# A decoder layer whose down projection is reordered feature by feature, with earlier weight fetches

## The chip, the cores and the metric

The kernel runs on one core of one Trainium2 chip. Its time is the device time of one execution in microseconds (us). Five engines work beside each other, each on its own queue of instructions in a fixed order: TensorE (PE in the profile; PEld is its weight load), VectorE (DVE), ScalarE (ACT), GpSimd (POOL) and SyncE (SP), which here only issues transfers (DMAs). GpSimd issues transfers too, those that add what they bring to what is there.

## The reference

The layer takes x (512 tokens of 1024 features, float32) and computes three sub-layers, each between two RMS norms: a SwiGLU feed-forward part, a token mixing part, and a second feed-forward part. The change touches the two feed-forward parts alone; cut to them the reference is:

```python
def swiglu(x, w_gu, w_down):                 # w_gu: 1024 x 5632, w_down: 2816 x 1024
    g, u = jnp.split(x @ w_gu, 2, axis=-1)
    return (jax.nn.silu(g) * u) @ w_down

h = h + 0.5 * rmsnorm(swiglu(rmsnorm(h, ffn1_pre_w), ffn1_w_gu, ffn1_w_down), ffn1_post_w)
u = rmsnorm(h, mix_pre_w)
h = h + rmsnorm(token_mixing(u, mem, ...), mix_post_w)       # untouched by the change
h = h + 0.5 * rmsnorm(swiglu(rmsnorm(h, ffn2_pre_w), ffn2_w_gu, ffn2_w_down), ffn2_post_w)
```

## The kernel before

**Precision.** TensorE is used with operands rounded to a short float32 form. Each operand is split in two, `hi` (a copy by ScalarE) and `lo` (the remainder, a subtraction by VectorE; `split`, L171 to L173), and each product is three matmuls, hi by hi, hi by lo, lo by hi (`mm3`, L377). So each 128x512 piece of a weight costs one ScalarE and one VectorE instruction before it can be used.

**A feed-forward part** (`ffn`, L713) has 22 groups of 128 hidden features ("features" below). The first two (EARLY) are computed in the plain way at the start ("heads"). The other 20 go in five *wides* of four. In a wide (`wide_pair`, L642) gate and up columns are computed with Strassen's scheme: the 2x2 block product is made of seven products, numbered 1 to 7 and run in the order 1, 6, 2, 5, 7, 4, 3, each of 24 matmuls of 512 columns (`wide_product`, L629). Their left operands are halves of the normalised x and sums of these (`xhi`, `xlo`, t1 to t4). Their right operands are blocks of w_gu or sums of blocks (`wide`, L584): products 1, 2 and 4 use blocks as loaded (tiles `st`, four buffers); products 5 and 7 use sums of two blocks, made by a plain load from SyncE and an accumulating one from GpSimd onto it (tiles `sum`, five buffers, `both`, L593); products 6 and 3 use a block of which VectorE adds one of these in place. Split pieces lie in 18 buffers `w`. The loads of a product are issued from up to four products before it.

**Turning.** The results of a wide have tokens in rows, and the down projection needs features in rows. `turn` (L694) does this for each of the four groups of 128 tokens: VectorE transposes 32x32 blocks (L698), a transfer writes to DRAM (L701), another reads back with rows exchanged (L704), and ScalarE and VectorE split the result (L709, L710). Before the change VectorE reads its input with a step of four elements, the write is one transfer of 128 rows, and the exchange of rows lies in the read.

**Down projection.** The features of one wide are multiplied by their rows of w_down during the next wide, between its products (`downs`, L807). For each half of the 1024 output columns it takes all (two or four) weight pieces of 128x512, each through one of two staging buffers `sh` and split into the common pool of 37 slots (names `s`), and then goes token group by token group: one of three PSUM banks `px`, all features of this group (3 matmuls each), and one addition to the result `y` by VectorE (for the first two features a copy by ScalarE). `DOWNS` (L44) says how many such steps follow each product, one row for common wides, one for the last wide of the second part, one for that of the first. The last features go behind the last wide with weights of their own (four in the second part; six in the first, where two of the wide before are kept back, `tail`), loaded as `st` and split into `w` buffers and into the places of t1 to t4, which are free by then (`spare`). Then the norm and the residual sum follow for each token group.

**What sets the order.** The kernel is a Python program that issues instructions in the order in which it runs; generators let steps of one task stand between those of another. A scheduler then fixes the order on each engine ahead of time: among the instructions that would be ready by its own estimate of durations, the one issued earliest by the program goes first. So an instruction can stand behind another that is late in fact. Loads go through `bring` (L148); right after the start the first nine are held in their order (`ordered`, L577). The beginning of the kernel (`open`, L464) is written out in a fixed order; there the reciprocal root of each norm is a GpSimd instruction (L194).

Of the kernel before, what the change touches and what calls it, by code (L numbers as in the profile page):

```python
# [8 lines left out]
F32 = mybir.dt.float32  # L9
# [34 lines left out]
DOWNS = ((0, 1, 1, 1, 2, 1, 2), (0, 1, 1, 1, 1, 1, 1), (0, 1, 1, 1, 1, 0, 0))  # L44
# [3 lines left out]
EARLY = 2  # L48
# [3 lines left out]
class Layer:  # L52
# [531 lines left out]
    def wide(self, w, c1, c2):  # L584


        k0 = w.rearrange("(k p) c -> p k c", p=P)
        raw, ops = {}, {}

        def quarter(j, h, c):  # L590
            raw[j] = [x[:, i, :] for x in (self.load(w, 4 * h + 2 * n, 2, c, 512) for n in range(2)) for i in range(2)]

        def both(j, h1, d1, h2, d2):  # L593
            raw[j] = []
            for k in range(4):
                u = self.wpool.tile([P, 512], F32, tag="sum", bufs=NSUM, name=f"sum{self.uid()}")
                self.bring(u, k0[:, 4 * h1 + k, d1:d1 + 512])
                self.nc.gpsimd.dma_start(out=u, in_=k0[:, 4 * h2 + k, d2:d2 + 512], accum_op=ALU.add)  # L598
# [95 lines left out]
    def turn(self, g, turned, t):  # L694
# [3 lines left out]
        self.nc.vector.transpose(blocks.rearrange("p (b f i) -> p f b i", b=4, f=4), g.rearrange("p (f j b) -> p f b j", f=4, b=4))  # L698
        n = self.uid()
        d = self.dram.tile([4, 32, 4, P], F32, tag=f"turn{n}", name=f"turn{n}")  # L700
        self.nc.sync.dma_start(out=d.rearrange("a j b x -> (a j) (b x)"), in_=blocks)  # L701
# [11 lines left out]
    def ffn(self, w_gu, w_down, w_post, ready, reload, after, early, last=False):  # L713
# [26 lines left out]
        def down_weights(f, hf):  # L740

            st = self.stage.tile([P, 512], F32, tag="st2", bufs=2, name=f"sh{self.uid()}")
            self.bring(st, w_down[f * P:(f + 1) * P, HALVES[hf]])
            return self.wsplit(st, slot=True)

        def down(t, hf, act, ws, first, bank=self.paux, cs=slice(0, 512)):
            acc = bank((P, cs.stop - cs.start))
            lhs = act(t)
            for k in range(len(ws)):
                self.mm3(acc, lhs[k], (ws[k][0][:, cs], ws[k][1][:, cs]), k == 0, k == len(ws) - 1)  # L750
            if first:
                nc.scalar.copy(y[t][hf], acc)
            else:
                self.tt(y[t][hf][:, cs], y[t][hf][:, cs], acc, ALU.add)

        wides = [self.wide(w_gu, f * P, DFF + f * P) for f in range(early, NF, 4)]
# [57 lines left out]
        tail = 0 if last else 2  # L814
        f0, n, act = 0, early, of_heads
        for s in range(len(wides)):
# [18 lines left out]
        ws, spare = [], list(self.spare())  # L835
        for j in range(n):
            st = self.load(w_down, f0 + j, 1, 0, D)
            ws.append([])
            for hf in range(2):
                i = j - 2 + (n - 2) * hf  # L840
                if j < 2 or i >= len(spare):
                    ws[-1].append(self.wsplit(st[:, 0, HALVES[hf]]))
                else:
                    self.split(*spare[i], st[:, 0, HALVES[hf]])
                    ws[-1].append(spare[i])
# [3 lines left out]
        if last:  # L849
            self.last_tiles(lambda t, hf, cs: down(t, hf, act, [w[hf] for w in ws], False, self.psum, cs), y, gain, h, after)  # L850
            return tasks
        for t in range(NT):
            whole, parts = slice(0, 512), (slice(0, 256), slice(256, 512))
            ss = []
            for hf in range(2):
                for cs in parts if hf == 1 and t == NT - 1 else (whole,):
                    down(t, hf, act, [w[hf] for w in ws], False, self.psum, cs)
# [692 lines left out]
```

## Time and profile before

| what | value |
|---|---|
| three runs | 1370.13, 1376.26, 1377.42 us (median 1376.26) |
| the profiled execution | 1378.38 us, its span 1376.6 us |
| mean granted clock of TensorE | 0.991 of full speed |
| busy: PE, DVE, ACT, POOL | 1324.1, 1053.1, 728.1, 94.8 us |
| matmuls | 7548 |
| bytes moved | 206.01 MB |

The first feed-forward part takes about the first 385 us of the span, the mixing the time up to about 1020 us, the second feed-forward part the rest. In the views a row of a timeline is: start and duration in us, engine, line, operation, written tile and the tiles it reads, shape, count, and in brackets the idle time of the engine before it with what ended that. "SPq" and "POOLq" are the issuing of transfers. Names such as s, w, st, sum, sh, px, ps are those of the tiles above, without their numbers (px and ps are PSUM).

### The profile page before, as it was taken

How to read it: one execution, taken by the hardware profiler on the slowest of the kernel's cores; microseconds unless marked ns; L12 is line 12 of the kernel's file. 1: busy time of each engine (PE TensorE's matmuls, PEld its weight loads, DVE VectorE, ACT ScalarE, POOL GpSimd, SP SyncE). 2: the span in 40 equal slices, each digit the busy share in tenths (PEclk: the TensorE clock that was granted, in tenths of full speed). 3: DMA queues.
4: the chain of work that ended last, by engine and by line, in shares of the span. 5: the costliest groups of instructions: out<-in, count | busy, mean ns of one | idle time of the engine just before them, and what ended most of it. 6: DMA issues, size and time to landing. Idle time of an engine off the chain costs nothing.

```text
span 1376.6 us, 21006 instructions
## 1 busy us (share of the span) xinstructions
PE 1324.1 (96%) x7548; PEld 1146.9 (83%) x7548; DVE 1053.1 (76%) x1911; ACT 728.1 (53%) x1457; POOL 94.8 (7%) x124
## 2 busy tenths in 40 slices
PE   7989899999899999999999999999999999999996
PEld 7867777778679898899889999999788877777785
DVE  5777768687799886599958978897577969586776
ACT  6555354444367765365765655565465644443442
POOL 2012020200010000000000000001001020101000
PEclk9999999999999999999999999999999999999998
DMA  9368384937725344343314333327625694857534
GB/s 269 100 184 227 126 225 128 243 123 192 253 77 142 121 129 145 106 133 110 106 47 123 95 99 93 111 90 184 214 92 133 180 253 121 231 157 194 154 115 161
DMA packets 190055, 206.01 MB, mean 150 GB/s; under 512 B 12761, under 2 KB 120702, under 8 KB 189950
## 3 DMA queue, kind: packets, MB, share of 16 engines
q1 hardware_dynamic: 174006, 180.47, 41.5%
q0 software_dynamic: 11520, 20.98, 9.2%
q10 hardware_dynamic: 4424, 3.22, 0.7%
q8 instruction: 59, 0.97, 0.3%
q14 instruction: 46, 0.38, 0.1%
HBM read 184.67 MB, written 19.96 MB: 149 GB/s over the span
## 4 chain that ended last, share of the span: by engine, by line
PE 58%; DVE 17%; DMA 15%; ACT 4%; issue 3%; POOL 1%; SPq 0%; POOLq 0%; DVEq 0%; ACTq 0%
PE ps L380 14%; PE ps L398 7%; PE ps L399 6%; PE ps L400 6%; PE px L380 6%; DVE s L167 6%; DVE w L167 4%; DMA sh<-in_ffn_w_down_dram 4%; PE ps L638 4%; PE ps L637 4%; PE ps L639 4%; PE px L385 4%; DMA sum<-in_ffn_w_gu_dram 3%; DVE s L698 2%; PE px L389 2%
## 5 line engine op out<-in xcount | busy, mean ns | idle before, releaser
L172 ACT ACTIVATE w<-st 128x512 fp32r<-128x512 f32 x360 | 219.8, 628 | 135.7 <-PE ps L638 52.1
L167 DVE TENSOR_TENSOR w<-st,w 128x512 fp32r<-128x512 f32 x368 | 245.4, 686 | 24.3 <-ACT w L172 21.4
L380 PE MATMUL px<-s,s 128*128 128x512 f32 x816 | 210.2, 397 | 24.0 <-ACT s L172 22.8
L167 DVE TENSOR_TENSOR w<-sum,w 128x512 fp32r<-128x512 f32 x208 | 142.2, 688 | 96.8 <-ACT w L172 93.4
L380 PEld LDWEIGHTS px<-s,s 128*128 128x128 f32 x816 | 152.5, 190 | 69.2 <-ACT s L172 31.4
L172 ACT ACTIVATE w<-sum 128x512 fp32r<-128x512 f32 x208 | 128.6, 631 | 135.3 <-DMA sum<-in_ffn_w_gu_dram 65.9
L167 DVE TENSOR_TENSOR s<-s,s 128x512 f32<-128x512 f32 (+3 forms) x277 | 169.5, 621 | 29.8 <-ACT s L672 17.4
L598 POOL DMA_DIRECT2D sum<-in_ffn_w_gu_dram x80 | 70.4, 949 | 876.8 <-DVE w L167 438.5
L167 DVE TENSOR_TENSOR s<-s,ps 128x256 f32<-128x256 f32 (+1 forms) x155 | 86.9, 560 | 32.4 <-PE ps L380 27.8
L398 PE MATMUL ps<-xhi,w 128*128 128x256 f32 x384 | 108.9, 284 | 0.0
L400 PE MATMUL ps<-xhi,w 128*128 128x256 f32 x384 | 108.7, 283 | 0.0
L399 PE MATMUL ps<-xlo,w 128*128 128x256 f32 x384 | 108.6, 283 | 0.0
L638 PE MATMUL ps<-w,xhi 128*128 128x512 f32 x240 | 93.9, 391 | 0.6 <-DVE w L167 0.6
L637 PE MATMUL ps<-w,xhi 128*128 128x512 f32 x240 | 93.5, 391 | 0.4 <-ACT w L172 0.4
L639 PE MATMUL ps<-w,xlo 128*128 128x512 f32 x240 | 93.5, 390 | 0.0
L380 PE MATMUL ps<-s,w 128*128 128x512 f32 (+1 forms) x384 | 80.2, 364 | 0.0
L380 PE MATMUL ps<-w,xhi 128*128 128x512 f32 x256 | 80.0, 393 | 0.0
L398 PEld LDWEIGHTS ps<-xhi,w 128*128 128x128 f32 x384 | 73.6, 192 | 0.7 <-ACT s L407 0.2
L399 PEld LDWEIGHTS ps<-xlo,w 128*128 128x128 f32 x384 | 73.6, 192 | 0.6
L380 PEld LDWEIGHTS ps<-s,w 128*128 128x128 f32 x384 | 65.0, 189 | 10.7
L400 PEld LDWEIGHTS ps<-xhi,w 128*128 128x128 f32 x384 | 73.6, 192 | 0.0
L172 ACT ACTIVATE s<-sh 128x512 fp32r<-128x512 f32 x68 | 42.8, 632 | 57.5 <-DMA sh<-in_ffn_w_down_dram 57.5
(234 smaller groups left out, 3081.5 us busy)
## 6 DMA issues: line engine op xcount, KB each, us to landing
st<-in_ffn_w_gu_dram SPq DMA_DIRECT2D x68, 512.0 KB, 5.2
st<-in_w_in_dram SPq DMA_DIRECT2D x48, 512.0 KB, 3.7
sum<-in_ffn_w_gu_dram SPq DMA_DIRECT2D x80, 256.0 KB, 5.3
sum<-in_ffn_w_gu_dram POOLq DMA_DIRECT2D x80, 256.0 KB, 6.5
sh<-in_ffn_w_down_dram SPq DMA_DIRECT2D x68, 256.0 KB, 4.1
turn<-s SPq DMA_DIRECT2D x40, 256.0 KB, 2.1
s<-turn SPq DMA_DIRECT2D x40, 256.0 KB, 2.8
sum<-in_w_in_dram SPq DMA_DIRECT2D x32, 256.0 KB, 3.2
```

What stands on the lines that cost most here:

```text
L167: ins = self.nc.vector.tensor_tensor(out=out, in0=a, in1=b, op=op)
L172: self.pin(self.nc.scalar.activation(hi, src, AF.Copy))
L380: self.pin_pe(mm(out, lhsT=lhs[l], rhs=rhs[r], start=a, stop=b))
L385: self.nc.tensor.matmul(out, lhsT=lhsT, rhs=rhs, start=start, stop=stop, **k)
L389: self.pin_pe(self.nc.tensor.transpose(out, in_, self.ident))
L398: mm(out, lhsT=lh, rhs=rh, start=first and k == 0, stop=False, skip_group_check=True)
L399: mm(out, lhsT=lh, rhs=rl, start=False, stop=False, skip_group_check=True)
L400: mm(out, lhsT=ll, rhs=rh, start=False, stop=k == 3, skip_group_check=True)
L598: self.nc.gpsimd.dma_start(out=u, in_=k0[:, 4 * h2 + k, d2:d2 + 512], accum_op=ALU.add)
L637: mm(banks[t], lhsT=lh, rhs=w[k][0], start=first and k == 0, stop=False, skip_group_check=True)
L638: mm(banks[t], lhsT=lh, rhs=w[k][1], start=False, stop=False, skip_group_check=True)
L639: mm(banks[t], lhsT=ll, rhs=w[k][0], start=False, stop=k == 3, skip_group_check=True)
```

## The change

Five edits, all of them in the feed-forward parts.

1. `downs` goes feature by feature: four banks (three `px` and one of the five `ps`) stay open for one half of the columns, each step multiplies one weight piece with all four token groups (12 matmuls), and the four additions to `y` follow together behind the half's last feature. The weight pieces are loaded straight into slots, three steps ahead (AHEAD), and split one step ahead.
2. In the first wide of each part (`first`) the operand of product 5 is no longer summed by the accumulating transfer. The second block is loaded by SyncE into the two staging buffers, and VectorE adds it.
3. The sum for product 3 is issued together with product 2's operands.
4. `turn` reads its input in order, writes with four transfers of 32 rows each in another order of rows, and reads back plainly.
5. `DOWNS` has other rows. One feature instead of two is kept back in the first part (TAIL). The last weights but two are loaded and split beside product 7 of the last wide, the other two behind it, and the products with them are made in that order.

The diff, cut to what the text speaks of:

```diff
-DOWNS = ((0, 1, 1, 1, 2, 1, 2), (0, 1, 1, 1, 1, 1, 1), (0, 1, 1, 1, 1, 0, 0))
+DOWNS = ((0, 0, 2, 2, 2, 1, 1), (0, 0, 2, 1, 1, 1, 1), (0, 0, 1, 1, 1, 1, 0), (0, 0, 1, 0, 1, 0, 0))
-EARLY = 2
+EARLY, TAIL, AHEAD = 2, 1, 3
...
-        def both(j, h1, d1, h2, d2):
+        def both(j, h1, d1, h2, d2, apart=False):
...
-                self.nc.gpsimd.dma_start(out=u, in_=k0[:, 4 * h2 + k, d2:d2 + 512], accum_op=ALU.add)
+                x = k0[:, 4 * h2 + k, d2:d2 + 512]
+                if apart:
+                    rest[j].append(self.stage.tile([P, 512], F32, tag="st2", bufs=2, name=f"sh{self.uid()}"))
+                    self.bring(rest[j][k], x)
+                else:
+                    self.nc.gpsimd.dma_start(out=u, in_=x, accum_op=ALU.add)
...
             elif j == 6:
-                both(5, 0, c2, 1, c2)
+                both(5, 0, c2, 1, c2, first)
...
             if j == 6:
+                for k, x in enumerate(rest[5]):
+                    self.tt(raw[5][k], raw[5][k], x, ALU.add)
                 for k in range(4):
                     self.tt(raw[1][k], raw[1][k], raw[5][k], ALU.add)
                 raw[6] = raw[1]
-            elif j == 3:
+            w = [self.wsplit(raw[j][k]) for k in range(4)]
+            if j == 2:
                 for k in range(4):
                     self.tt(raw[2][k], raw[2][k], raw[6][k], ALU.add)
                 raw[3] = raw[2]
-            return [self.wsplit(raw[j][k]) for k in range(4)]
+            return w
...
-        self.nc.vector.transpose(blocks.rearrange("p (b f i) -> p f b i", b=4, f=4), g.rearrange("p (f j b) -> p f b j", f=4, b=4))
+        self.nc.vector.transpose(blocks.rearrange("p (b f i) -> p f b i", b=4, f=4), g.rearrange("p (f b j) -> p f b j", f=4, b=4))
...
-        self.nc.sync.dma_start(out=d.rearrange("a j b x -> (a j) (b x)"), in_=blocks)
+        for a in range(4):
+            self.nc.sync.dma_start(out=d.rearrange("b j a x -> a j b x")[a], in_=blocks[32 * a:32 * a + 32, :].rearrange("j (b x) -> j b x", b=4))
...
-        self.nc.sync.dma_start(out=swapped.rearrange("p (a x) -> p a x", a=4), in_=d.rearrange("a j b x -> (j b) a x"))
+        self.nc.sync.dma_start(out=swapped, in_=d.rearrange("b j a x -> (b j) (a x)"))
...
         def downs(f0, n, act):
-            for hf in range(2):
-                ws = [down_weights(f0 + f, hf) for f in range(n)]
+            todo, ws = [(hf, f) for hf in range(2) for f in range(n)], {}
+
+            def load(i):
+                hf, f = todo[i]
+                ws[i] = self.slot()
+                self.bring(ws[i], w_down[(f0 + f) * P:(f0 + f + 1) * P, HALVES[hf]])
+
+            def make(i):
+                ws[i] = self.wsplit(ws[i], slot=True)
+
+            for i in range(AHEAD):
+                load(i)
+            make(0)
+            for i, (hf, f) in enumerate(todo):
+                yield
+                if i + AHEAD < len(todo):
+                    load(i + AHEAD)
+                if i + 1 < len(todo):
+                    make(i + 1)
+                if f == 0:
+                    acc = [self.paux() if t < 3 else self.psum() for t in range(NT)]
                 for t in range(NT):
-                    yield
-                    down(t, hf, act, ws, f0 == 0)
+                    self.mm3(acc[t], act(t)[f], ws[i], f == 0, f == n - 1)
+                for t in range(NT if f == n - 1 else 0):
+                    if f0:
+                        self.tt(y[t][hf], y[t][hf], acc[t], ALU.add)
+                    else:
+                        nc.scalar.copy(y[t][hf], acc[t])
...
-            for j, m in enumerate(DOWNS[2 if end and tail else 1 if end else 0]):
+            for j, m in enumerate(DOWNS[tail + 1 if end else 0]):
                 if j or s or not resumed:
                     next(pair, None)
-                for _ in range(m + (j == 0)):
+                if end and j == 4:
+                    final(range(2, 4 + tail))
+                for _ in range(m + (j == 1)):
                     next(behind, None)
```

More of the change, by code (lines that the diff above doesn't have):

```diff
@@ L738, in new_act, with down @@
             return self.slot(dt=F32R), self.slot(dt=F32R)
[L740 to L747, printed above, removed]
-            lhs = act(t)
[L749 to L756, printed above, removed]
+        def down(t, hf, cs):
+            acc = self.psum((P, cs.stop - cs.start))
+            order = [*range(2, n), 0, 1]
+            lhs = act(t)
+            for k in order:
+                self.mm3(acc, lhs[k], [x[:, cs] for x in ws[k, hf]], k == 2, k == 1)
+            self.tt(y[t][hf][:, cs], y[t][hf][:, cs], acc, ALU.add)
+        wides = [self.wide(w_gu, f * P, DFF + f * P, f == early) for f in range(early, NF, 4)]
         todo = [(s, j) for s in range(len(wides)) for j in (1, 6, 2, 5, 7, 4, 3)]
@@ L833, in ffn @@
         f0, n = f0 + n - tail, 4 + tail
[L835 to L845, printed above, removed]
+        final(range(2))
         h = reload()
@@ L849, in ffn @@
         if last:
-            self.last_tiles(lambda t, hf, cs: down(t, hf, act, [w[hf] for w in ws], False, self.psum, cs), y, gain, h, after)
+            self.last_tiles(down, y, gain, h, after)
             return tasks
@@ L856, in ffn @@
                 for cs in parts if hf == 1 and t == NT - 1 else (whole,):
-                    down(t, hf, act, [w[hf] for w in ws], False, self.psum, cs)
+                    down(t, hf, cs)
                     ss.append(self.square(y[t][hf][:, cs], hf, 0.5))
```

18 lines of the change are left out of this document (14 added, 4 removed).

## The prediction

> **What bounds the kernel now.** I read the page first, then the sums by stretch, then who TensorE waits for.
>
> ```profile
> PE 1324.1 (96%) x7548; PEld 1146.9 (83%) x7548; DVE 1053.1 (76%) x1911; ACT 728.1 (53%) x1457; POOL 94.8 (7%) x124
> ```
>
> TensorE bounds it: 96% of the span busy, the others far less. What can be gained is its idle time. By stretch (length; PE, PEld, DVE, ACT, POOL busy; granted clock; DMA):
>
> ```profile
> 52.00:340.00 288.00, 273.38 (x1164) 219.03 (x1163) 210.78 (x339) 136.93 (x244) 30.59 (x36) 0.98 0.65 180
> 1085.00:1345.00 260.00, 250.75 (x1089) 202.32 (x1088) 196.96 (x307) 118.12 (x209) 23.49 (x27) 1.00 0.60 171
> ```
>
> The wides idle for 14.6 us in the first feed-forward part and 9.3 us in the second. TensorE's waits over the whole span (total us, times, longest):
>
> ```profile
> PE px L380 <- ACT s L172: 22.8, 17, 4.1
> PE px L389 <- DVE s L499: 4.8, 2, 3.5
> PE ps L380 <- DVE s L167: 1.8, 2, 1.5
> PE px L380 <- DVE s L167: 1.1, 1, 1.1
> PE ps L380 <- ACT s L709: 0.9, 1, 0.9
> ```
>
> The first row is the down projection waiting for a split weight piece: 22.8 of the 23.9 us that the wides idle. How it comes about, from one timeline:
>
> ```profile
> 1164.88 1.54 SPq L154 DMA_DIRECT2D sh<-in_ffn_w_down_dram  x2
> 1168.24 0.63 ACT L172 ACTIVATE s<-sh 128x512 fp32r<-128x512 f32 x1 [2.43 <-DMA sh<-in_ffn_w_down_dram]
> 1168.92 0.50 PE L380 MATMUL px<-s,s 128*128 128x512 f32 x1 [0.88 <-ACT s L172]
> ```
>
> The third of four pieces is loaded only once the first has left its staging buffer; it lands 3.4 us later, is split at once, and TensorE is already there, since a token group wants all four pieces within 12 matmuls. Long waits cost twice: the clock behind four of them (same columns as above) is
>
> ```profile
> 26.00:30.00 4.00, 4.00 (x22) 3.79 (x23) 3.12 (x7) 2.26 (x5) 0.74 (x1) 0.57 1.09 250
> 84.00:88.50 4.50, 4.50 (x14) 3.54 (x13) 1.94 (x4) 0.56 (x2) 0.00 (x0) 0.62 1.02 318
> 147.50:152.00 4.50, 4.50 (x11) 3.54 (x12) 1.54 (x3) 0.39 (x1) 0.00 (x0) 0.50 0.36 117
> 357.00:361.00 4.00, 3.99 (x11) 3.14 (x12) 3.06 (x5) 0.00 (x0) 0.00 (x0) 0.57 1.00 311
> ```
>
> Length times the missing share gives 1.7, 1.7, 2.25 and 1.7 us, 7.4 in all. The ceiling of the change is so 23.9 + 3.5 (the longer wait on L499) + 2.4 (0.9 on L709 and 1.5 on L167, both behind the last wide of the first part) + 7.4 = 37.2 us.
>
> **The change part by part.** *Down projection by feature.* The same matmuls. One takes 0.227 us:
>
> ```profile
> 1212.39 5.60 PE L380 MATMUL px<-s,s 128*128 128x512 f32 x24
> 1217.83 0.39 PE L637 MATMUL ps<-w,xhi 128*128 128x512 f32 x1
> ```
>
> (5.44 us / 24), so one piece now feeds 12 matmuls, 2.72 us, and is split one such step ahead. Each of the 17 waits can shrink by 2.72 us. Two are longer, 4.14 and 3.31:
>
> ```profile
> 147.32 0.80 PE L380 MATMUL px<-s,s 128*128 128x512 f32 x1 [4.14 <-ACT s L172]
> 83.63 0.50 PE L380 MATMUL px<-s,s 128*128 128x512 f32 x1 [3.31 <-ACT s L172]
> ```
>
> They leave 1.4 + 0.6 = 2.0 us: 23.9 - 2.0 = 21.9 gained, and with them the two clock losses at 84 and 147 us, 3.95. Bounds: 0 (the order of ScalarE, below) to 27.9. The staging buffers no longer hold SyncE back; a load waits for a free slot instead, but at a time 3 raw and 4 split slots are in use where a half took 8, so I add no wait for slots. PSUM: with one `ps` bank lent, a wide has four, and never needs more at once (two pairs open); the lent banks are emptied by four additions, 2.4 us by the 0.6 us from one VectorE start to the next, under a product of 5.44 us. Nothing for both; if that cover were gone, 2.4 us per half.
>
> *First sum by VectorE.* At the start the reciprocal root for the last token group stands in GpSimd's queue behind two accumulating transfers, which wait for their base to land:
>
> ```profile
> 19.71 0.21 DVE L191 TENSOR_SCALAR v<-ss,ss 128x1 f32<-128x1 f32 x1
> 22.45 1.95 POOL L598 DMA_DIRECT2D sum<-in_ffn_w_gu_dram  x2 [6.18 <-DMA sum<-in_ffn_w_gu_dram]
> 23.75 1.23 POOL L194 TENSOR_TENSOR r<-v,mhalf 128x1 f32<-128x1 f32 x1
> ```
>
> Without them it can run at 20 instead of 23.75; TensorE's 3.5 us and the clock's 1.7 go: 5.2. But the third and fourth second blocks need the two staging buffers, so their loads wait for VectorE's first additions, and the product 2 loads are held behind them in SyncE's order. VectorE reaches product 6's sums here, and TensorE product 6 there:
>
> ```profile
> 44.63 0.68 DVE L167 TENSOR_TENSOR st<-st,sum 128x512 f32<-128x512 f32 x1
> 48.70 0.61 PE L637 MATMUL ps<-w,t2hi 128*128 128x512 f32 x2
> sum<-in_ffn_w_gu_dram SPq DMA_DIRECT2D x80, 256.0 KB, 5.3
> ```
>
> Both move 5.2 earlier: first addition at 39.4, load issued at 40.1, landed 5.3 later at 45.4, two additions and a split (0.6, 0.6, 0.6, 0.7) until 47.9, wanted 6 matmuls after 43.5, at 44.9. So 3.0 late if VectorE does not slip the additions in earlier, 0 if it does. I take 2.0, nearer the late end because VectorE is full there. Net gain 3.2 (bounds 0 to 5.2). In the second part no norm waits and VectorE has room: nothing.
>
> *Turning.* A transposition against an addition of the same shape, and one write's issue (duration min/median/max, ns):
>
> ```profile
> L698 DVE STREAM_TRANSPOSE s<-s 128x512 f32<-128x512 f32 x40 | 43.4, 1085 | 0.3
> L167 DVE TENSOR_TENSOR s<-s,s 128x512 f32<-128x512 f32 x143 | 96.8, 686 | 21.3 <-ACT s L672 17.4 <-ACT s L689 2.2 <-DMA s<-in_ffn_post_w_dram 1.5
> L701 SPq DMA_DIRECT2D turn<-s x40: 319/320/339, 91.3 to 1343.3; - x40
> ```
>
> Between 0 and 0.4 us of VectorE time per turn is gained, 16 us over 40, and three issues of 0.32 us, 0.96, are added, with the loads queued behind them. Before, a turn's last instruction was
>
> ```profile
> 1225.15 0.69 DVE L167 TENSOR_TENSOR s<-s,s 128x512 fp32r<-128x512 f32 x1 [0.35 <-ACT s L709]
> ```
>
> done at 1225.84, 13.3 us behind product 3's last matmul (about 1212.5). The new first step wants all four groups after 12 + 72 matmuls, 19.05 us. With 0.96 more, 4.8 us remain: nothing on the path.
>
> Why the transposition is slow the trace cannot say. The Trainium skill ("SBUF — State Buffer", Door 1) says that accesses which leave a 16-byte line each time pay a penalty; the old read steps exactly 16 bytes, so by it the 0.4 us go, and if transposing itself costs it, nothing does. The time is the same by both, only the room in a rival below differs.
>
> *Last weights, one feature kept back, order.* Behind product 3 the first part's last turns are late because VectorE first splits last weights:
>
> ```profile
> 325.81 5.74 SPq L154 DMA_DIRECT2D st<-in_ffn_w_down_dram  x4
> 345.85 0.63 ACT L172 ACTIVATE t1hi<-st 128x512 fp32r<-128x512 f32 x1 [3.16 <-DMA st<-in_ffn_w_down_dram]
> 347.72 0.68 DVE L167 TENSOR_TENSOR s<-s,ps 128x512 f32<-128x512 f32 x1
> ```
>
> With ten splits instead of twelve, six of them moved ahead, the addition at 347.72 can run some 4.4 us earlier (at 343.3, without the pair loaded last). But two token groups give 12 matmuls less cover (2.7), and beginning with the new features instead of the two held takes 1.4 more. I take 1.0 gained (bounds -4.1 to +4.1). SyncE passes nothing new: four of these loads stood ahead of products 4 and 3 before (325.81), three do now; and the splits' places, t1 to t3, are free after product 7. The second part's end has no wait of TensorE and stays. The earlier sum for product 3 frees two `st` buffers sooner and costs no instruction.
>
> *What is late next.* The wide weights. ScalarE already waits for summed blocks:
>
> ```profile
> ACT w L172 <- DMA sum<-in_ffn_w_gu_dram: 65.9, 21, 6.9
> ```
>
> I put 3 us of new waits there (bounds 0 to 15), low because two steps (24 matmuls) now stand between products 5 and 7 instead of one.
>
> Sum: 21.9 + 3.95 + 3.2 + 1.0 - 3 = 27.1 off the profiled execution's 1378.4: **1351 us**. That execution is 2 us above the median of the runs, inside their spread, so I leave the figure.
>
> **The rivals.** *All goes*, no new waits: 1378.4 - 37.2 = 1341. For it: ScalarE and VectorE idle for 47% and 24% of the span. Against: data that is late is rarely late in one place.
>
> *VectorE delays the wide weights.* From product 3 to the next product 6 it is nearly full:
>
> ```profile
> 1207.00:1229.00 22.00, 22.00 (x99) 18.22 (x98) 20.82 (x33) 11.67 (x21) 0.00 (x0) 1.00 0.34 106
> ```
>
> That stretch shrinks from 96 to 84 matmuls, 19.05 us, for 20.8 us of VectorE work: 1.8 late per wide if the transpositions stay as slow, 0.2 if they gain 1.6. Over the eight wides that follow another, 1.8 costs 14.4 in place of the 3: 1362. Against it: four additions to y among that work, 2.4 us, can be put off.
>
> *ScalarE's order holds the pieces back, not their loading* (the change doesn't do what it says). At 83.6 us it was so:
>
> ```profile
> 81.94 0.63 ACT L172 ACTIVATE w<-st 128x512 fp32r<-128x512 f32 x1 [2.50 <-DMA st<-in_ffn_w_gu_dram]
> 82.94 1.15 ACT L172 ACTIVATE s<-sh 128x512 fp32r<-128x512 f32 x2
> ```
>
> The pieces were there (no wait stands before their split at 82.9), but ScalarE had just waited for a wide weight that was late. If all 17 waits are of this kind and stay, only the opening and the end gain, 4.2, against the 3: 1377, no change. Against it: in the row at 1168.24 it is the piece itself that lands late.
>
> *The turn comes late for the first step* (slower). The four writes of a turn run one after the other instead of overlapping. A write lands 2.1 us after its issue, so four take 8.4. The last two turns of a wide are issued 3.5 us apart (the pair's 3.81 less one issue),
>
> ```profile
> turn<-s SPq DMA_DIRECT2D x40, 256.0 KB, 2.1
> 1216.10 3.81 SPq L701 DMA_DIRECT2D turn<-s  x2
> ```
>
> so the second's writes begin at 1224.5, when the first's are through, and end at 1232.9 instead of 1221.7: ready 11.2 later, 24.5 us behind product 3 where 19.05 are covered. 5.4 us of wait and 1.85 of slow clock (the mean of the four above) in each of eight wides are 58 us: 1409. It decides from 27.1 / 8 = 3.4 us per wide on, that is a turn ready 22.4 us behind product 3. Against it: transfers of one queue overlap in this trace,
>
> ```profile
> s<-h SPq DMA_DIRECT2D x16, 256.0 KB, 5.5
> 1345.77 4.12 SPq L144 DMA_DIRECT2D s<-h  x8
> ```
>
> eight loads issued within 4.1 us, less than one takes to land. The Trainium skill ("DMA: Bandwidth & Descriptors", Rules for kernel authors) is on the rival's side: it tells to use one transfer of 128 partitions, as transfers to separate partition ranges serialize, and that under 64 KB one pays mostly overhead; these pieces are 64 KB. No run here shows such writes of 32 rows.
>
> **How the numbers follow.** My forecast, 1351, has a chance of 0.49 (its own range 1342 to 1361); all goes 0.10; VectorE 0.17, since it is the fullest engine beside TensorE; ScalarE's order 0.14, as one of the two longest waits shows it; the late turn 0.10, against the overlap seen. Under 0.5%, 6.9 us, a measurement of this kernel can't tell from no change. Faster are the first three, 0.76; the same 0.14; slower 0.10. The range goes from 1338 (the ceiling, less 0.4 us for each of the eight turns that end the two parts) to 1376, which leaves the late turn and half of ScalarE's order outside, and a little below: 0.2.
>
> **What would show it.** Down projection right: the row of px behind ScalarE falls from 22.8 to under 5 us, and the granted clock at about 84 and 147 us is full. First sum right: the wait on L499 near 26 us falls under 1 us; my doubt shows as a wait of up to 3 us of product 6 near 44 us. Turning: L698 near 0.7 us or still 1.09. What is late next shows as L637 and L638 waiting for ScalarE or VectorE. The prediction is wrong if px still waits for ScalarE as before, or if the first step of a wide waits for L709, the turn.

## The result, and the profile after

The changed kernel takes 1447.37 us (median of four runs, 1444.36 to 1449.67) against 1374.78 us (1370.13 to 1377.42). The ratio is 1.0531, 95% interval 1.0493 to 1.0568: slower by 73 us, where 27 us faster were predicted, and far above the range. The profiled execution after has a span of 1442.6 us, 66.0 more than before. Its page's line of busy times, and the main waits of TensorE (total us, times, longest):

```profile
PE 1334.9 (93%) x7545; PEld 1158.4 (80%) x7545; DVE 1045.6 (72%) x1919; ACT 732.4 (51%) x1457; POOL 88.5 (6%) x116
```

```profile
PE px L380 <- ACT s L172: 80.9, 13, 9.9
PE ps L646 <- DVE w L167: 3.1, 3, 2.3
PE ps L645 <- ACT s L658: 2.6, 3, 1.1
PE px L380 <- DVE s L167: 2.5, 6, 1.0
...
PE px L389 <- DVE s L499: 2.1, 2, 1.3
```

PE is busy 10.8 us longer (1334.9 - 1324.1) for the same work: its mean granted clock is 0.968 where it was 0.991. It is idle 55.2 us longer (the rest of the 66.0), and the first row alone covers that: TensorE waits for a split piece of w_down for 80.9 us, where it was 22.8. The row that was to fall under 5 has more than tripled. By the timelines, 69.6 of the 80.9 us are eight stops of 5.4 to 9.9 us, one in each wide that follows another, in front of its first down step.

One common wide of the second part, from its product 5 to the next one's, before (first row) and after (length; PE, PEld, DVE, ACT, POOL busy; granted clock; DMA share; GB/s):

```profile
1177.70:1241.50 63.80, 61.00 (x265) 49.00 (x264) 47.42 (x74) 28.42 (x50) 6.96 (x8) 1.00 0.65 182
```

```profile
1230.50:1302.10 71.60, 62.04 (x266) 50.63 (x265) 46.24 (x74) 28.66 (x50) 6.97 (x8) 0.93 0.62 159
```

A common wide takes 7.8 us more. Its idle time (length less PE busy) was 2.8 us, at several pieces, and is now 9.6 us, all at one place, the first down step, which stands behind product 2. This is the timeline of the changed kernel at the same place one wide earlier (TensorE, ScalarE, then the issues of SyncE and GpSimd), and the same stretches as windows:

```profile
1223.34 1.22 PE L380 MATMUL px<-s,s 128*128 128x512 f32 x2 [9.42 <-ACT s L172]
...
1211.69 0.61 ACT L172 ACTIVATE w<-sum 128x512 fp32r<-128x512 f32 x1
1220.86 0.63 ACT L172 ACTIVATE w<-sum 128x512 fp32r<-128x512 f32 x1 [8.56 <-DMA sum<-in_ffn_w_gu_dram]
1222.14 0.63 ACT L172 ACTIVATE w<-sum 128x512 fp32r<-128x512 f32 x1 [0.66 <-DMA sum<-in_ffn_w_gu_dram]
1222.68 0.61 ACT L172 ACTIVATE s<-s 128x512 fp32r<-128x512 f32 x1
...
1207.02 0.34 SPq L713 DMA_DIRECT2D s<-turn  x1
1208.21 1.53 SPq L154 DMA_DIRECT2D sum<-in_ffn_w_gu_dram  x3
...
1210.27 1.47 SPq L154 DMA_DIRECT2D s<-in_ffn_w_down_dram  x3
...
1212.79 2.68 POOL L603 DMA_DIRECT2D sum<-in_ffn_w_gu_dram  x3 [49.16 <-DVE s L167]
```

```profile
1213.90:1223.30 9.40, 0.02 (x1) 0.00 (x0) 1.19 (x2) 1.78 (x3) 3.30 (x4) 0.64 1.02 250
1223.40:1228.00 4.60, 4.60 (x14) 3.66 (x15) 3.27 (x6) 3.16 (x6) 0.66 (x1) 0.64 1.00 279
```

Read it from the bottom. Product 2 ends at 1213.9. SyncE issues the three down pieces from 1210.27 on, behind three loads for product 7's sums. The first piece lands 6.3 us after its issue (the first row below, the view of issues cut to this one; the second row is the page's median), at about 1216.6, already 2.7 us late. ScalarE doesn't split it then: in its order two splits of product 7's sums stand ahead, and the first of these sums is complete only at 1220.86, since GpSimd's accumulating halves left at 1212.79 and the DMA engines are full (share 1.02). The piece is split at 1222.68, 6.1 us after it landed, though nobody needs product 7's sums before that step. TensorE has idled for 9.4 us, and its next 4.6 us run at a clock of 0.64.

```profile
s<-in_ffn_w_down_dram SPq DMA_DIRECT2D x1, 256.0 KB, 6.3
s<-in_ffn_w_down_dram SPq DMA_DIRECT2D x70, 256.0 KB, 6.2
turn<-s SPq DMA_DIRECT2D x160, 64.0 KB, 1.8
```

What was announced for the other parts came. The stretch at 26 us (its row before had a clock of 0.57) runs at full clock, by the view by stretch:

```profile
26.00:30.00 4.00, 4.00 (x35) 4.00 (x34) 3.17 (x7) 3.00 (x6) 0.00 (x0) 1.00 0.01 4
```

Product 6 waits at 47 us as doubted, by the timeline, and the transposition is faster, by its line's own view (duration min/median/max in ns, first and last start):

```profile
47.13 0.50 PE L646 MATMUL ps<-w,t2hi 128*128 128x512 f32 x1 [2.26 <-DVE w L167]
```

```profile
L706 DVE STREAM_TRANSPOSE s<-s x40: 698/705/712, 88.6 to 1406.1; 128x512 f32<-128x512 f32 x40
```

### The profile page after: what moved, and what is told of

It reads as the page before. It is cut to its first block, busy times and chain, and to the rows that moved or that the text cites. A ratio compares the mean times of both kernels' runs of the same rounds, so it can differ in the third digit from the quotient of the medians.

```text
span 1442.6 us, 21171 instructions
## 1 busy us (share of the span) xinstructions
PE 1334.9 (93%) x7545; PEld 1158.4 (80%) x7545; DVE 1045.6 (72%) x1919; ACT 732.4 (51%) x1457; POOL 88.5 (6%) x116
## 4 chain that ended last, share of the span: by engine, by line
PE 69%; DMA 11%; DVE 11%; ACT 4%; issue 3%; POOL 1%; SPq 1%; POOLq 0%; DVEq 0%; ACTq 0%
PE ps L380 18%; PE px L380 9%; DMA sum<-in_ffn_w_gu_dram 7%; PE ps L398 6%; PE ps L400 6%; PE ps L399 6%; PE ps L646 6%; PE ps L645 6%; PE ps L647 6%; DVE s L167 4%; PE px L385 4%; DVE w L167 3%; PE px L389 1%; DMA s<-turn 1%; ACT w L172 1%
## 5 line engine op out<-in xcount | busy, mean ns | idle before, releaser
L172 ACT ACTIVATE w<-st 128x512 fp32r<-128x512 f32 x360 | 224.1, 630 | 175.1 <-PE ps L646 90.6
L380 PE MATMUL px<-s,s 128*128 128x512 f32 x630 | 177.5, 425 | 83.4 <-ACT s L172 80.9
L167 DVE TENSOR_TENSOR s<-s,s 128x512 fp32r<-128x512 f32 (+3 forms) x347 | 215.4, 633 | 53.0 <-ACT s L680 27.2
L380 PEld LDWEIGHTS px<-s,s 128*128 128x128 f32 x630 | 128.2, 207 | 121.6 <-ACT s L172 87.0
L603 POOL DMA_DIRECT2D sum<-in_ffn_w_gu_dram x72 | 63.6, 978 | 919.4 <-DVE s L167 585.6
L167 DVE TENSOR_TENSOR s<-s,ps 128x512 f32<-128x512 f32 (+1 forms) x171 | 96.6, 572 | 30.4 <-PE ps L380 24.9
L167 DVE TENSOR_TENSOR sum<-sum,st 128x512 f32<-128x512 f32 x96 | 65.3, 685 | 2.3 <-DMA st<-in_w_in_dram 1.9
```

The source lines that it names most:

```text
L167: ins = self.nc.vector.tensor_tensor(out=out, in0=a, in1=b, op=op)
L172: self.pin(self.nc.scalar.activation(hi, src, AF.Copy))
L380: self.pin_pe(mm(out, lhsT=lhs[l], rhs=rhs[r], start=a, stop=b))
L603: self.nc.gpsimd.dma_start(out=u, in_=x, accum_op=ALU.add)
```

## The experiments

Ratios are to the kernel before, run on the same chip beside them (its medians there lay between 1374.7 and 1376.7 us). "Lead" is how far ahead of its step a piece is asked for. Steps are "bunched" in the changed kernel's `DOWNS` rows, where two often follow one product, and "spread" in the rows of before, where mostly one does. "Old turn" and "old rows" are those of the kernel before.

| run | what | us | ratio, interval |
|---|---|---|---|
| e1_lead | change, pieces and first split after product 1 | 1398.1 | 1.0149 [1.0114, 1.0185] |
| e9_load_early | change, pieces alone after product 1 | 1398.4 | 1.0160 [1.0125, 1.0195] |
| e17_sums_later | change, product 7's sums fetched later | 1447.5 | 1.0513 [1.0469, 1.0558] |
| e2_spread | e1 with the old rows of steps | 1369.5 | 0.9951 [0.9931, 0.9970] |
| e3_oneturn | change with the old turn | 1411.6 | 1.0256 [1.0221, 1.0291] |
| e14_lead_oneturn | e1 with the old turn | 1392.3 | 1.0126 [1.0085, 1.0167] |
| e7_spread_oneturn | e2 with the old turn | 1367.7 | 0.9948 [0.9930, 0.9966] |
| e5_turn | before with the new turn | 1397.2 | 1.0173 [1.0135, 1.0210] |
| e10_four_writes | before with the four writes | 1402.3 | 1.0181 [1.0146, 1.0216] |
| e11_transpose | before with the new transposition; tokens come out in another order | 1367.9 | 0.9935 [0.9908, 0.9961] |
| e15_tiny_writes | before with three tiny transfers more per turn | 1374.6 | 0.9994 [0.9971, 1.0017] |
| e6_sums | before with the new sums | 1375.0 | 0.9996 [0.9973, 1.0019] |
| e4_sumturn | before with new sums and new turn | 1394.2 | 1.0133 [1.0097, 1.0170] |
| e8_spread_sum3 | e2 with the old place of product 3's sum | 1384.0 | 1.0077 [1.0051, 1.0103] |
| e13_feature_only | before with the projection by feature | 1375.6 | 1.0000 [0.9977, 1.0023] |
| e12_earlier | e2, pieces ahead of product 1, shorter last row | 1361.5 | 0.9894 [0.9859, 0.9928] |
| e16_split_two | e12, split two steps ahead | 1374.9 | 0.9988 [0.9968, 1.0008] |
| e18_earlier_oneturn | e12 with the old turn | 1374.6 | 0.9986 [0.9965, 1.0007] |

### When the first pieces are asked for, and how the steps stand

```diff
 e1_lead (to the changed kernel)
-                for _ in range(m + (j == 1)):
+                for _ in range(m + (j == 0)):
 e2_spread (to e1_lead)
-DOWNS = ((0, 0, 2, 2, 2, 1, 1), (0, 0, 2, 1, 1, 1, 1), (0, 0, 1, 1, 1, 1, 0), (0, 0, 1, 0, 1, 0, 0))
+DOWNS = ((0, 1, 1, 1, 2, 1, 2), (0, 1, 1, 1, 1, 1, 1), (0, 1, 1, 1, 1, 0, 0), (0, 1, 1, 1, 1, 0, 0))
```

> The changed kernel with one thing put back: the down projection's first three loads and first split are written after product 1 of a wide, as before the change, not after product 6. Theory (lead): in the changed kernel TensorE stands some 9.5 us at the first down step of a full wide, because the first piece is asked for behind the loads of product 7's sums on SyncE and split behind their splits on ScalarE; with one product (5.4 us) more of lead that wait goes or falls to 4 us or less per wide, the row of px behind ScalarE's split falls from 80.9 us to below 30, and the time from 1447 to 1365 to 1395. Rival (slots): the loads now wait for free slots, so asking earlier only moves the wait; px stays above 60 us and the time above 1425. Rival (bunching): two steps stand together after product 2 and a step gives 2.7 us where a load and split need 7.5, so half of the loss stays: 1400 to 1425.

> As the run before, and also the steps spread over the products as before the change (the first step after product 6, one after most products, two after the fifth and the last). Theory (lead): little is added to the run before, since what was missing was the lead; within 10 us of it, and a first step right after product 6 has only 5.4 us again, so it may be up to 15 us slower. Rival (bunching): the pairs of steps were the loss; then this one is faster than the run before by 15 us or more.

One product of lead takes 49 us off, and px behind ScalarE falls to 31.7 us, just above the 30 expected; the time lies between the ranges of the lead and of the bunching.

```profile
PE px L380 <- ACT s L172: 31.7, 12, 4.8
```

Spreading the steps takes 29 more, so the bunching rival holds for the rest, and the kernel is then faster than before by 0.5%. (The edit changes all four rows, the ends of the parts too.) The late first pieces and the bunching are two losses side by side. The common wide (same columns as above) of e1 and then e2:

```profile
1195.60:1259.80 64.20, 62.19 (x265) 50.49 (x264) 46.16 (x74) 28.43 (x50) 6.80 (x8) 0.97 0.67 180
```

```profile
1175.70:1236.30 60.60, 60.52 (x265) 49.21 (x264) 46.08 (x74) 28.28 (x50) 6.85 (x8) 1.00 0.70 190
```

With spread steps a wide takes 60.6 us; its 264 matmuls of 0.227 us are 59.9. The common wide has next to nothing left to win. Next: is it the load or the split that was too late in its order?

```diff
 e9_load_early (to the changed kernel)
             for i in range(AHEAD):
                 load(i)
+            yield
             make(0)
...
-                for _ in range(m + (j == 1)):
+                for _ in range(m + (j <= 1)):
 e17_sums_later (to the changed kernel)
-                upto = todo.index((s, j)) + 4
+                upto = todo.index((s, j)) + (3 if j == 6 else 4)
```

> The changed kernel with the down projection's first three loads written after product 1, as before the change, but its first split left after product 6. Theory (ScalarE's order): in the changed kernel the piece had landed some 6 us before ScalarE came to it, since two splits of product 7's sums stood ahead and waited for their transfers; earlier loading doesn't help then: px behind ScalarE stays above 60 us, the time above 1425. Rival (SyncE's order): the loads stood behind the loads of the sums, and asking earlier is what helped before (1398): below 1410, px below 40 us.

My theory fell: moving the loads alone gives all that e1 gave. The split, still written after product 6, was put elsewhere by the scheduler. Issues of SyncE and ScalarE in e9:

```profile
1185.99 0.34 SPq L713 DMA_DIRECT2D s<-turn  x1
1186.39 1.38 SPq L154 DMA_DIRECT2D s<-in_ffn_w_down_dram  x3
1187.87 1.32 SPq L154 DMA_DIRECT2D sum<-in_ffn_w_gu_dram  x3
...
1191.19 0.63 ACT L172 ACTIVATE s<-s 128x512 fp32r<-128x512 f32 x1 [0.49 <-DMA s<-in_ffn_w_down_dram]
...
1201.26 0.63 ACT L172 ACTIVATE w<-sum 128x512 fp32r<-128x512 f32 x1 [6.69 <-DMA sum<-in_ffn_w_gu_dram]
```

The pieces now stand ahead of the three sum loads on SyncE, and the split ahead of the three splits on ScalarE that wait for these sums. So two orders flip together once the loads are written one product earlier. ScalarE still stands 6.69 us for product 7's sums, but behind the piece, and TensorE doesn't stop for it. Does it suffice to write the sums later instead?

> The changed kernel with one thing moved: at product 6 only three products ahead are fetched instead of four, so that the loads of product 7's sums are written behind the down projection's first three loads, not ahead of them. The piece itself is asked for after product 6 as in the change. Theory (what stands ahead): of the 9.4 us of wait at the first step some 6 are ScalarE standing on product 7's sums and some 3.5 the plain lead; 5.5 us and the slow clock for seven wides go: 1395 to 1412 against 1447. Rival (plain lead): the wait stays near 9 us: 1435 or more. Further possibility: product 7 itself now waits for its sums.

Nothing moved. But the order didn't either: SyncE still issues the sums first,

```profile
1209.21 1.53 SPq L154 DMA_DIRECT2D sum<-in_ffn_w_gu_dram  x3
...
1211.27 1.53 SPq L154 DMA_DIRECT2D s<-in_ffn_w_down_dram  x3
```

although the program writes them behind the pieces. The run is no proof for the rival, whose number it met: it shows that the written order alone does not bind the scheduler, and leaves open what in its estimate holds the pieces back (a free slot, for one).

How the 9.4 us divide can be estimated from the changed kernel's trace. The piece waited 6.1 us, from its landing at 1216.6 to its split at 1222.68. Split at once, it would have let TensorE start 0.66 us later (1223.34 - 1222.68), so about 3.3 us of the stop are the late landing and 6.1 us are ScalarE's order.

The kernel e2 points the same way, that the order counts for more than the lead. There the loads are written one product ahead of the first step, as in the changed kernel (and in the kernel before), but ahead of product 7's sums. In its common wide the piece is split 4.0 us after its issue, as soon as it lands, and TensorE doesn't stop (SyncE, ScalarE, TensorE):

```profile
1163.75 1.41 SPq L154 DMA_DIRECT2D s<-in_ffn_w_down_dram  x3
1165.27 1.93 SPq L154 DMA_DIRECT2D sum<-in_ffn_w_gu_dram  x3
...
1167.75 0.63 ACT L172 ACTIVATE s<-s 128x512 fp32r<-128x512 f32 x1 [1.97 <-DMA s<-in_ffn_w_down_dram]
...
1168.54 0.86 PE L380 MATMUL px<-s,s 128*128 128x512 f32 x3
```

### The turn

```diff
 e5_turn (to before): the whole of turn as in the change; e3_oneturn, e14_lead_oneturn, e7_spread_oneturn: turn as before
 e10_four_writes (to before)
-        self.nc.sync.dma_start(out=d.rearrange("a j b x -> (a j) (b x)"), in_=blocks)
+        for a in range(4):
+            self.nc.sync.dma_start(out=d.rearrange("a j b x -> a j (b x)")[a], in_=blocks[32 * a:32 * a + 32, :])
 e11_transpose (to before)
-g.rearrange("p (f j b) -> p f b j", f=4, b=4)
+g.rearrange("p (f b j) -> p f b j", f=4, b=4)
 e15_tiny_writes (to before, behind the one write)
+        rest = self.dram.tile([3, 16], F32, tag=f"rest{n}", name=f"rest{n}")
+        for a in range(3):
+            self.nc.sync.dma_start(out=rest[a:a + 1, :], in_=blocks[32 * a:32 * a + 1, 0:16])
```

> The changed kernel with the old turn: transposition from 16-byte steps, one write of 128 rows in place of four of 32, and the read-back in pieces. Theory (lead): the turn has nothing to do with the loss; 1440 to 1455, and px behind ScalarE near 81 us. Rival (queue): the three more issues per turn on SyncE hold the down loads back; then this one is 20 us or more below 1447.

> The changed kernel with the first loads behind product 1, its bunched steps, and the old turn. Theory (one cost: too little time between asking for a piece and its step, which the four writes lengthen): with one write the bunched steps lose less, 1370 to 1385 (with four writes 1398, with spread steps 1368). Rival (two costs): bunching costs 28 us with either turn, so 1393 to 1400.

> The changed kernel with the down projection's first loads after product 1, its steps spread as before the change, and the old turn. Theory (turn costs wherever it stands): 17 to 36 us less than with the new turn, 1333 to 1353 against 1370, so well below the 1376 of before. Rival (the cost of the turn belongs to the late first piece): with the piece asked for early the turn no longer matters, 1364 to 1375.

> The kernel before with the new turn alone (other read order of the transposition, four writes of 32 rows, whole read-back). With the sums by VectorE it was 17 us slower than before, and the changed kernel with the old turn was 36 us faster than with the new one. Theory (turn): the four writes per token group keep SyncE's order longer and push the wide's other loads back; alone it costs most of the 17 us: 1387 to 1397 against 1376. Rival (sums): the turn alone costs nothing or gains up to 5 us, 1371 to 1380, and the 17 us come from the sums.

The queue rival's number came in e3, 36 us below the change (its reason is tried below), and the turn alone costs 22.6 us in the kernel before (e5). But with the lead restored it costs 6 (1398.1 to 1392.3), and 2 with spread steps (1369.5 to 1367.7, intervals overlapping). Spread or bunched is 25 to 29 us with either turn (e14 to e7, e1 to e2), so those are two costs, as e14's rival said. Which part of the turn?

> The kernel before with its turn's write split into four transfers of 32 rows, all else of the turn as before (the new turn as a whole cost 22.6 us). Theory (the three more issues): they alone put other loads further back in SyncE's order: 1390 to 1402 against 1375. Rival (other parts of the turn): 1370 to 1380.

> The kernel before with the transposition reading its input in order and nothing else of the turn changed; the tokens then come out in another order, so this prices the instruction and leaves the exchange of rows wrong. Theory (the three more issues): VectorE is freed of 0.4 us per turn and the rest stays, 1368 to 1376. Rival (the earlier turn itself moves other work): 1385 or more.

> The kernel before with its one write per turn, and three more transfers of 64 bytes each behind it into memory that nothing reads. Theory (issues and order): the loads of the down pieces fall behind the sums' loads in SyncE's order as with four writes, and the time is 1390 to 1402. Rival (the transfers of 32 rows): the order stays, 1374 to 1382.

The four writes cost 26 us (1402.33 - 1376.48), and the transposition by itself gains 8.6 (0.65%): 0.38 us less of VectorE per turn is worth something after all, by VectorE's room or by the earlier turn. With 23 for the whole turn these don't add up, and the plain read-back was not tried alone. Three more issues alone cost nothing, against my theory. SyncE's order shows the difference (loads of `st` left out). Before:

```profile
1220.01 2.02 SPq L704 DMA_DIRECT2D s<-turn  x2
1226.47 0.34 SPq L154 DMA_DIRECT2D sum<-in_ffn_w_gu_dram  x1
...
1228.28 1.54 SPq L154 DMA_DIRECT2D sh<-in_ffn_w_down_dram  x2
```

With four writes:

```profile
1230.10 0.38 SPq L705 DMA_DIRECT2D s<-turn  x1
...
1232.40 0.36 SPq L705 DMA_DIRECT2D s<-turn  x1
1233.59 0.35 SPq L154 DMA_DIRECT2D sum<-in_ffn_w_gu_dram  x1
...
1235.67 3.34 SPq L154 DMA_DIRECT2D sum<-in_ffn_w_gu_dram  x4
1240.48 1.85 SPq L154 DMA_DIRECT2D sh<-in_ffn_w_down_dram  x2
```

With three tiny transfers:

```profile
1211.45 1.12 SPq L707 DMA_DIRECT2D s<-turn  x2
...
1216.44 0.35 SPq L154 DMA_DIRECT2D sum<-in_ffn_w_gu_dram  x1
1218.85 0.35 SPq L154 DMA_DIRECT2D sh<-in_ffn_w_down_dram  x1
```

The down pieces (`sh`) stand behind one sum load before and with the tiny transfers, 8.3 and 7.4 us after the first read-back; with four writes they stand behind five, 10.4 us after it. The read-back has to wait for all four writes and for none of the tiny ones, and the loads stand in another order. Whether the scheduler's estimate or the writes' own time does it is not settled; that the order changed, and that three more issues by themselves cost nothing, is shown. That the order is the whole price is not shown: of the 19.7 us by which e10's profiled execution is longer, 8.6 are TensorE's wait for split pieces (31.4 against 22.8), 3.3 its other idle time and 7.8 its busy time, at a mean clock of 0.985 against 0.991.

### The sums

```diff
 e6_sums (to before): wide() as in the change; e4_sumturn: turn() as well
 e8_spread_sum3 (to e2_spread)
-            w = [self.wsplit(raw[j][k]) for k in range(4)]
-            if j == 2:
+            elif j == 3:
...
-            return w
+            return [self.wsplit(raw[j][k]) for k in range(4)]
```

> The kernel before with the sums alone (first wide's sums for products 5 and 6 by VectorE; sums for product 3 behind product 2's splits). Theory (turn): only the opening moves: 1370 to 1376. Rival (sums): taking the sums for product 3 forward puts four additions ahead of other work of VectorE in every wide and frees buffers in another order: 1387 to 1397.

> The kernel before with two of the changes alone: the first wide's sums for products 5 and 6 by VectorE, with the sums for product 3 behind product 2's splits, and the turn with four writes. The down projection and the last weights are as before. Theory: what the changed kernel showed at 26 us (stall and slow clock gone, 5.2 us) less the 2.3 us of product 6 at 47 us, and the turn at nothing: 1368 to 1374, against 1375 before. Rival: these two parts carry some of the loss of 73 us: above 1385.

> The changed kernel with the first loads after product 1 and spread steps, and with the sums for product 3 taken where they were before the change (with product 3's splits, not behind product 2's). Theory (turn): the sums' place is worth little, 1364 to 1375 against 1370. Rival (sums): below 1358.

In the order of before the sums are worth nothing (e6), so e4's loss is the turn's (e5 has it too). In the order of e2 the old place of product 3's sum is 14 us slower: the theory had put that place at little, and the rival had even hoped for a gain. The same edit has another price in another order.

### By feature alone, and the fastest version

```diff
 e13_feature_only (to before): downs() of the change with AHEAD = 3, the rest as before
 e12_earlier (to e2_spread)
             for i in range(AHEAD):
                 load(i)
+            yield
             make(0)
...
+            next(behind)
             for j, m in enumerate(DOWNS[tail + 1 if end else 0]):
...
-(0, 1, 1, 1, 1, 0, 0), (0, 1, 1, 1, 1, 0, 0))
+(0, 1, 1, 1, 0, 0, 0), (0, 1, 1, 1, 0, 0, 0))
 e16_split_two (to e12_earlier)
             make(0)
+            make(1)
...
-                if i + 1 < len(todo):
-                    make(i + 1)
+                if i + 2 < len(todo):
+                    make(i + 2)
 e18_earlier_oneturn (to e12_earlier): turn as before
```

> The kernel before with the down projection by feature alone: loads three ahead into slots, the first ones behind product 1, steps in the rows of before, two features kept back as before, old turn, old sums. Theory (the term was right, its place in the order wrong): in the common wides px no longer waits for ScalarE, some 2.8 us per wide and the slow clock go, less new waits of 5 to 7 us at the first pieces of the two second wides: 1355 to 1368 against 1376. Rival (by feature is itself the loss): 1380 or more.

Between the two: no gain and no loss. A common wide of e13, and TensorE's main waits there:

```profile
1175.80:1237.20 61.40, 60.49 (x266) 49.44 (x265) 47.25 (x74) 27.73 (x50) 7.13 (x9) 1.00 0.66 190
```

```profile
PE px L380 <- ACT s L172: 11.7, 4, 4.5
PE ps L380 <- DVE s L167: 7.5, 4, 4.0
PE px L380 <- DVE s L167: 6.2, 7, 0.9
```

The common wide gains 2.4 us (63.80 to 61.40), most of its 2.8 us of idle time. The px row behind ScalarE falls from 22.8 to 11.7, but the rows behind VectorE rise by 10.8 (1.8 and 1.1 before, 7.5 and 6.2 now), so the three together hardly change. Most of what is left stands where no common wide stands: 4.5 and 4.3 us at the first pieces of the two second wides, 6.9 at the end of the first part, 2.6 in the last wide of the second.

> The changed kernel with spread steps (1369.5), and with the first three loads of a wide's down projection written ahead of its product 1, the first split behind product 1, and one step more left for behind the last wide (rows 0, 1, 1, 1, 0, 0, 0 in the first part). There TensorE stood 7.1 us at 112 us, 6.2 us at 1104 us for a first piece and 9.1 us behind the first part's last wide, each with slow clock behind. Theory (lead): the first two go, and the end loses about 4: 1345 to 1357. Rival (order or slots): the loads are put off anyway and come no earlier: 1364 or more.

> The run of 1361.5 us (first loads ahead of product 1, spread steps) with the pieces split two steps ahead instead of one. Theory (late splits): the 5.4 us of px behind ScalarE at the first part's end go, and 1 to 2 us of slow clock: 1352 to 1358. Rival (the turns of the last wide are late in any case, since VectorE stands behind the mixing's first weights there): 1359 to 1364. Loss through more slots held: above 1366.

> The run of 1361.5 us (first loads ahead of product 1, spread steps) with the old turn. Theory (beside spread steps the turn costs nothing either way): 1356 to 1366. Rival (fewer writes shorten the end of the first part, where 9 us of waits are left): 1346 to 1355. Rival (VectorE, 16 us fuller by the slower transposition): above 1368.

e12 is the fastest, 1.06% below before. The stops in front of a second wide's first step, which in e2 were 7.1 us in the first part (its timeline below) and 6.2 in the second, fell to 2 us each:

```profile
112.45 0.80 PE L380 MATMUL px<-s,s 128*128 128x512 f32 x1 [7.07 <-ACT s L172]
```

The end of the first part kept its 9 us (timeline of e12),

```profile
338.23 1.65 PE L380 MATMUL px<-s,s 128*128 128x512 f32 x3 [5.40 <-ACT s L172]
343.52 2.93 PE L380 MATMUL px<-s,s 128*128 128x512 f32 x6 [3.64 <-DVE s L167]
```

so it landed 4.5 us above the theory. Splitting further ahead (e16) was 13 us slower, although px behind ScalarE fell from 6.0 to 2.3 us: in all eight wides that follow another TensorE now waits for ScalarE's copies of product 1. In a common wide of e16 the copies stand behind five splits of sums on ScalarE, in e12 behind three; why the scheduler ordered them so is open. That row of the waits, in e12 and then in e16:

```profile
PE ps L645 <- ACT s L658: 4.1, 2, 2.1
```

```profile
PE ps L645 <- ACT s L658: 15.4, 8, 2.1
```

And beside this order the old turn is 13 us slower than the new (e18, in the range of its last rival; TensorE's px waits behind VectorE double from 8.1 to 16.2 us, those behind ScalarE from 6.0 to 11.7). The turn's price so runs from +36 us in the changed kernel over +23 in the kernel before to -13 here.

## Why the prediction was wrong

**The step that failed** is "each of the 17 waits can shrink by 2.72", with the bounds "0 to 27.9". It counts the time between a split and its use, and takes for granted that loads and splits come as early as before. But the title's "earlier weight fetches" is not true of the first three pieces of each wide: the change writes their loads one product later (`j == 0` became `j == 1`), behind the loads of product 7's sums, and I gave this no term, not even a bound below nothing. It costs 49 us (e1, e9). The bunching of the steps in the new rows had no term either; it costs 25 to 29 (e14 to e7, e1 to e2). The term itself measured 0, give or take 3, in place of 21.9 + 3.95 (e13): its gain in the common wides is real, and was given back at the second wides and at the two parts' ends. (The 21.9 also counts 1.1 us of idle time that is not in the 17 waits, 23.9 less 22.8.) These three, 49, 29 and 26 us, are 104 where the forecast was off by 96 (1447 against 1351); they were measured in different orders and need not add up.

**Turning**, put at nothing, is the second failure. The step "with 0.96 more, 4.8 us remain: nothing on the path" asked only whether the turn reaches its first step in time, which it did: no wait of the changed kernel's TensorE is for ScalarE's split of a turn. "The loads queued behind them" were named and not priced. In the order of before the four writes cost 26 us, the transposition gains 9, and the whole turn costs 23. The Trainium skill ("DMA: Bandwidth & Descriptors", Rules for kernel authors) tells to use one transfer of 128 partitions, since two transfers to disjoint partition halves serialize. The advice was right in the order of before, but its reason doesn't show: each 64 KB write landed 1.8 us after its issue, with the next ones issued some 0.43 us apart. The Trainium skill ("SBUF — State Buffer", Door 1) says that each access which crosses to a new 16-byte line pays a penalty. The trace agrees: 1085 ns fell to 705.

**First sum**, 3.2 net: the mechanism is right in both halves (the clock at 26 us, 2.26 us at product 6 where I put 2.0). With the earlier sum for product 3 beside it, it measured between 3.7 us gained and 2.6 lost (e6), which does not tell 3.2 from nothing. **Last weights**, 1.0, were not tried alone. **What is late next**, 3 us: the rows of `ps` behind w and behind ScalarE's copy are 5.7 us, of which 2.26 are the wait at product 6 just named; the rest, 3.4, is near it.

**The rivals.** "ScalarE's order holds the pieces back" named the engine, but it let the waits stay as they were; they went from 1.3 us on average (22.8 / 17) to 6.2 (80.9 / 13). "The turn comes late" had the right sign for a wrong reason: the writes overlap, and the first step waits for a weight. "VectorE delays the wide weights" is hardly seen: `ps` waits 3.1 us in all for VectorE's part of a split.

## What to carry to other kernels

Where a scheduler fixes each engine's order ahead of time, price a change first by where its loads and their first uses come to stand in the queues, against the loads of everything else, and only then by the cover of each step. A piece that falls behind work needed later can lose more than its own lateness: here a landing about 3 us late became a stop of 9.4, since the split stood behind two others that waited for their loads. With the same one product of lead but ahead of that work (e2), it lost nothing in the common wides. One edit's price measured in one order (the turn: +36, +23, -13 us) says little of its price in another, so try edits together with the order they will live in.

## What the runs showed of the hardware

Splitting one 256 KB write into four of 64 KB leaves each landing 1.8 us after its issue (one write: 2.1), with the next ones in flight. The same transposition of 128x512 takes 0.705 us when it reads its input in order and 1.085 us when it reads with a step of 16 bytes. A stop of 9.4 us is followed by 4.6 us of TensorE at a mean clock of 0.64; in the kernel before, stops of 1.5 to 4.1 us were followed by 4 to 4.5 us at 0.50 to 0.62.
